# Splitting the second layer's projection weights in quarters between the projections, and GpSimd's residual steps one turn later

## The chip, the cores and the metric

The kernel runs on one core of a Trainium2 chip. The core's engines are TensorE (PE; its weight loads are listed as PEld), VectorE (DVE), ScalarE (ACT) and GpSimd (POOL); SyncE's queue (SP) issues most transfers. Each engine works through its own queue in order, and the engines wait for one another by semaphores. The metric is the device time of one execution in microseconds (us).

## The reference, cut to what matters

The network is a two-layer diffusion block on 256 latent and 256 context tokens of 1024 features. The second layer (i = 1) starts with a windowed attention with 16 query heads and 4 key/value heads of 64 features. The part that matters here is its input projection:

```python
q_lat, k_lat, v_lat = jnp.split(u_lat @ w_in, [q_cols, q_cols + kv_cols], axis=-1)
k_ctx, v_ctx = jnp.split(u_ctx @ w_in[:, q_cols:], [kv_cols], axis=-1)
q_lat = apply_axial_rope(qh(q_lat), rope_cos, rope_sin)
k_lat = apply_axial_rope(kvh(k_lat), rope_cos, rope_sin)
```

The rope is `x1 * cos - x2 * sin` and `x2 * cos + x1 * sin`. All of it is wanted in float32.

## The kernel before, in words

**Three products for one.** TensorE is given each float32 operand as a rounded high part and the rest: `mm3` (L411 to L413) multiplies high by high, high by low and low by high and adds the three in PSUM. A weight chunk `w` of 128x2048 is therefore split: ScalarE writes the high part `wh` by a copy into the rounded type (L390), VectorE subtracts it from `w` into `wl` (L391). Both come in two buffers, `wh0`/`wh1` and `wl0`/`wl1`, used in turn.

**The stage.** `inproj1` computes the projections of the second layer. The values come first. Then a loop over five chunks c (keys for c = 0, two groups of query heads for each of c = 1 to 4) runs two projections each, e = 0 and 1. A projection (`proj`) is eight k-tiles of three matmuls; k-tile kt reads columns kt*256 to kt*256+255 of the chunk, so a quarter of a chunk (512 columns) holds two k-tiles. For c = 0 a matmul is 512 wide (context and latent tokens), for the others 256.

**What follows a projection.** ScalarE moves the result out of PSUM with a scale (L2203, into `pexp`). One projection later `pend` runs the finish: for keys `k_finish`, for queries `q_finish`. A finish begins with `rope`: TensorE multiplies the moved result with a rotation matrix (L2120, into `tp`), VectorE multiplies `tp` with the sines (L2122), GpSimd the moved result with the cosines (L2123), VectorE adds the two (L2125). Then ScalarE writes the high part of the outcome (L2154 and L2155 for keys, eight pieces; L2163 for queries, two pieces) and VectorE the low part (L2157, eight pieces; L2168, two pieces). The finishes of chunk 4 are put off into the attention that follows.

**Other work in the same turns.** After each e = 1 projection `self.ada(1)` multiplies one more chunk of the modulation weights (L480 on TensorE). `steps` is a list of ten GpSimd instructions on the residual rows `N` (two of L2184, eight of L2188), which are given out two per projection.

**What sets the order.** No scheduler: instructions stand on each engine in the order in which the Python code emits them. A raw weight buffer goes back to the free list in `release`, which at once issues the next load of a fixed stream on SP's queue (`pump`, L323); that load waits there for the last reader of the buffer, and the loads behind it wait too.

Of the kernel before, what the change touches and what calls it, by code (L numbers as in the profile page):

```python
# [11 lines left out]
F32 = mybir.dt.float32  # L12
# [4 lines left out]
OP = mybir.AluOpType  # L17
# [254 lines left out]
class Kern:  # L272
# [108 lines left out]
    def split(self, pool=False, n=1, bufs=None, low=False):  # L381

        w = self.take()
        h, l = bufs or (self.part("wh"), self.part("wl"))
        for i in range(n):
            s = slice(i * 2048 // n, (i + 1) * 2048 // n)
            if pool:
                self.nc.gpsimd.tensor_scalar(h[:, s], w[:, s], 1.0, 0.0, op0=OP.mult, op1=OP.add)
            else:
                self.nc.scalar.copy(h[:, s], w[:, s])  # L390
            (self.nc.gpsimd if pool or low else self.nc.vector).tensor_tensor(l[:, s], w[:, s], h[:, s].bitcast(F32), op=OP.subtract)  # L391
        self.release()
        return h, l

    def split_steps(self, n):

        w, held = self.take(), self.held
        h, l = self.part("wh"), self.part("wl")
        for i in range(n):
            s = slice(i * 2048 // n, (i + 1) * 2048 // n)  # L400
            self.nc.gpsimd.tensor_scalar(h[:, s], w[:, s], 1.0, 0.0, op0=OP.mult, op1=OP.add)  # L401
            self.nc.gpsimd.tensor_tensor(l[:, s], w[:, s], h[:, s].bitcast(F32), op=OP.subtract)
            if i == n - 1:
                self.wq.append((h, l))
                self.release(held)
            yield
# [1704 lines left out]
    def inproj1(self, u1):  # L2111
        nc, W, d = self.nc, self.W, self.d
        cos, sin = self.rope[:, 0], self.rope[:, 1]
        rpm = self.cb[:, C_RPM:C_RPM + 128]
        lat = slice(256, 512)
        v = self.area(4, [4, 256])

        def rope(dst, src, t2=None):
            p = self.tp()
            nc.tensor.matmul(p[:, :256], rpm, src, start=True, stop=True)  # L2120
            t2 = W.tile([128, 512], F32, name="pT", bufs=4)[:, :256] if t2 is None else t2
            nc.vector.tensor_tensor(t2, p[:, :256], sin, op=OP.mult)  # L2122
            nc.gpsimd.tensor_tensor(dst, src, cos, op=OP.mult)  # L2123
            yield
            nc.vector.tensor_tensor(dst, dst, t2, op=OP.add)  # L2125
            yield

        w = self.wq.pop(0)
        for t in u1:
            uh, ul = self.uh, self.ul  # L2130
            p = self.mm()
            ts = slice(t * 128, t * 128 + 128)
            for kt in range(8):
                sl = slice(kt * 256, kt * 256 + 256)
                self.mm3(p[:, :256], (uh[kt // 4][:, kt % 4, ts], ul[kt // 4][:, kt % 4, ts]), (w[0][:, sl], w[1][:, sl]),
                         kt == 0, kt == 7)
            nc.scalar.copy(v[:, t, :], p[:, :256])

        def proj(w, off, s):
            p = self.mm()  # L2140
            for kt in range(8):
                sl = slice(kt * 256 + off, kt * 256 + off + 128)
                self.mm3(p[:, :s.stop - s.start], (w[0][:, sl], w[1][:, sl]), (uh[kt // 4][:, kt % 4, s], ul[kt // 4][:, kt % 4, s]),
                         kt == 0, kt == 7)
            return p

        def k_finish(i, s):
            r = W.tile([128, 512], F32, name="pT", bufs=4)[:, :256]
            list(rope(r, s[:, 256:512]))
            for gl in range(2):  # L2150
                g = 2 * i + gl
                q, o = slice(64 * gl, 64 * gl + 64), slice(64 - 64 * gl, 128 - 64 * gl)
                for src, ks in ((s[q, 0:256], slice(0, 256)), (r[q], lat)):
                    nc.scalar.copy(kh[q, g, ks], src)  # L2154
                    nc.scalar.copy(kh[o, g, ks], src)  # L2155
                    for dst in (q, o):
                        nc.vector.tensor_tensor(kl[dst, g, ks], src, kh[q, g, ks].bitcast(F32), op=OP.subtract)  # L2157

        def q_finish(i, s, r=None, t2=None):
            r = W.tile([128, 512], F32, name="pT", bufs=4)[:, :256] if r is None else r  # L2160
            yield from rope(r, s, t2)
            for e in range(2):
                nc.scalar.copy(q2[i // 4][64 * e:64 * e + 64, i % 4, e], r[64 * e:64 * e + 64])  # L2163
            yield
            for e in range(2):
                q, o = slice(64 * e, 64 * e + 64), slice(64 - 64 * e, 128 - 64 * e)
                z = q2[i // 4][:, i % 4, e]
                nc.vector.tensor_tensor(z[o], r[q], z[q].bitcast(F32), op=OP.subtract)  # L2168
            yield

        kh = self.area(2, [4, 512], F32R)
        kl = self.area(3, [4, 512], F32R)
        q2 = [self.area(h, [4, 2, 256], F32R) for h in range(2)]
        nxt = self.wq.pop(0)
        self.table(AF.Exp)

        steps = []
        for h in range(2):
            hs = slice(h * 512, h * 512 + 512)
            gb = self.nt(h).rearrange("p (i n) -> p i n", i=2)  # L2180
            for i, name in enumerate(("ln_g", "ln_b")):
                a = d[name][0, 1, hs]
                nc.scalar.dma_start(gb[:, i], bass.AP(tensor=a.tensor, offset=a.offset, ap=[[0, 128], [1, 512]]))
            steps.append(lambda gb=gb: nc.gpsimd.tensor_scalar(gb, gb, ALPHA, 0.0, op0=OP.mult, op1=OP.add))  # L2184
            for row in (2, 3):
                n = self.nt(row)[:, hs]
                for x, op in ((gb[:, 0], OP.mult), (gb[:, 1], OP.add)):
                    steps.append(lambda n=n, x=x, op=op: nc.gpsimd.tensor_tensor(n, n, x, op=op))  # L2188
        pend, ends = None, []
        for c in range(5):  # L2190
            w = nxt
            if c < 4:
                nxt = self.split(n=4)
            for e in range(2):
                i = 2 * (c - 1) + e
                p = proj(w, e * 128, slice(0, 512) if c == 0 else lat)
                if c < 4:
                    s = W.tile([128, 512], F32, name="pexp", bufs=5)
                    s = s if c == 0 else s[:, :256]
                else:  # L2200
                    o = W.tile([128, 1024], F32, name=("gm", "bm")[e])
                    s, r, t2 = (o[:, 256 * k:256 * k + 256] for k in range(3))
                nc.scalar.mul(s, p[:, :s.shape[1]], 0.125 if c else 1.0)  # L2203
                if e:
                    self.ada(ADA_IN1[c])
                if pend:
                    pend()
                    pend = None
                for f in steps[:2] if c else []:
                    f()  # L2210
                del steps[:2 if c else 0]
                if c == 0:
                    pend = lambda i=e, s=s: k_finish(i, s)
                elif c < 4:
                    pend = lambda i=i, s=s: list(q_finish(i, s))
                else:

                    ends.append(q_finish(i, s, r, t2))
        assert not steps
        return q2, kh, kl, v, chain(*ends)  # L2220
# [373 lines left out]
```

## Time and profile before

| | |
|---|---|
| three runs | 798.36 us median (797.3 to 800.5) |
| profiled execution | 796.03 us, of which its span, first to last instruction, is 794.2 us |
| mean granted TensorE clock | 0.955 of full speed |
| busy over the span | PE 708.4, DVE 465.5, ACT 278.5, POOL 231.4 us |
| the stage of the change | 493 to 545 us |

Busy times overlap, and a matmul's end is modelled, so the share of TensorE is not its efficiency. A wait counts only where the engine that waits is the one that the end depends on.

### The profile page before, as it was taken

What the parts mean: (1) busy time and instruction counts of PE and PEld (TensorE: products, weight loads), DVE (VectorE), ACT (ScalarE), POOL (GpSimd) and SP (SyncE); (2) the same over time, 40 slices, a digit from 0 to 9 for tenths busy, and PEclk for the clock granted to TensorE, in tenths of its full rate; (3) what the DMA queues carried; (4) which work ended last, traced back from release to release, by engine and by line L of the source; (5) the groups of instructions that cost most, each with busy time, mean ns of one, the idle gap of its engine ahead of it and who ended that gap; (6) DMA issues with size and microseconds to landing.
All of it is one profiled execution on the core that took longest, in us unless ns stands there. A gap on an engine that the chain in (4) does not pass through costs nothing. (4 is left out here: it accounts for less than half of the span.)

```text
span 794.2 us, 11447 instructions
## 1 busy us (share of the span) xinstructions
PE 708.4 (89%) x4162; PEld 413.5 (52%) x4162; DVE 465.5 (59%) x1000; ACT 278.5 (35%) x611; POOL 231.4 (29%) x250
## 2 busy tenths in 40 slices
PE   4799999979989987999999787979999978899993
PEld 0477676724567764433433247765556744454430
DVE  0589897747754877723334386587676388322115
ACT  0541212036775254110110246455768342111121
POOL 1200000037632002844000192462486540111111
PEclk8799999969999997999999999999999997999997
DMA  9974665557458368999997932557464394996892
GB/s 360 389 286 169 241 236 202 222 205 266 141 181 338 116 225 304 385 363 349 410 415 305 394 126 93 172 212 311 181 250 159 134 385 169 422 375 258 348 375 84
DMA packets 36253, 209.66 MB, mean 264 GB/s; under 512 B 4439, under 2 KB 4695, under 8 KB 15056
## 3 DMA queue, kind: packets, MB, share of 16 engines
q1 hardware_dynamic: 27888, 183.56, 59.9%
q10 hardware_dynamic: 4816, 13.85, 5.3%
q0 software_dynamic: 3472, 11.31, 3.9%
q8 instruction: 37, 0.61, 0.3%
q14 instruction: 40, 0.33, 0.1%
HBM read 197.92 MB, written 12.06 MB: 264 GB/s over the span
## 5 line engine op out<-in xcount | busy, mean ns | idle before, releaser
L631 DVE SCALAR_TENSOR_TENSOR x<-x,sm,x 128x512 f32<-128x512 f32 x120 | 90.7, 756 | 3.4
L411 PE MATMUL mm<-H,wh 128*128 128x512 f32 (+1 forms) x208 | 78.5, 377 | 1.9 <-ACT H L614 1.9
L413 PE MATMUL mm<-H,wl 128*128 128x512 f32 (+1 forms) x208 | 76.2, 366 | 0.2 <-DVE wl L391 0.2
L412 PE MATMUL mm<-L,wh 128*128 128x512 f32 (+1 forms) x208 | 76.2, 366 | 0.1
L480 PE MATMUL aux<-w,sc 128*32 128x512 f32 x368 | 54.7, 689 | 16.8 <-ACT sc L444 7.6
L391 DVE TENSOR_TENSOR wl<-w,wh 128x512 fp32r<-128x512 f32 (+1 forms) x27 | 40.0, 1515 | 22.9 <-ACT wh L390 22.7
L401 POOL TENSOR_SCALAR wh<-w 128x256 fp32r<-128x256 f32 x32 | 13.2, 413 | 118.2 <-DMA w<-wo 118.1
L411 PEld LDWEIGHTS mm<-H,wh 128*128 128x128 f32 x208 | 40.3, 194 | 13.6 <-issue 3.4
L699 DVE TENSOR_REDUCE mx<-mm 128x1 f32<-128x512 f32 (+1 forms) x64 | 39.3, 615 | 13.3 <-PE mm L786 7.3
L1836 POOL TENSOR_TENSOR yl<-ada,yh 128x512 fp32r<-128x512 f32 x12 | 15.3, 1274 | 104.6 <-ACT yh L1833 104.6
L412 PEld LDWEIGHTS mm<-L,wh 128*128 128x128 f32 x208 | 40.3, 194 | 7.4 <-DVE L L617 1.0
L413 PEld LDWEIGHTS mm<-H,wl 128*128 128x128 f32 x208 | 40.1, 193 | 7.3 <-DVE wl L391 0.8
L411 PE MATMUL mm<-wh,H 128*128 128x512 f32 x104 | 43.2, 415 | 0.0
L723 ACT COPY pT<-tp 128x512 f32<-128x512 f32 (+1 forms) x64 | 33.9, 530 | 25.4 <-PE tp L721 25.1
L412 PE MATMUL mm<-wl,H 128*128 128x512 f32 x104 | 41.1, 395 | 0.0
L1402 PE MATMUL aux<-x,H 128*32 128x512 f32 (+2 forms) x104 | 38.6, 612 | 0.0
L1508 DVE TENSOR_TENSOR y<-mm,y 128x512 f32<-128x512 f32 x18 | 12.3, 690 | 41.7 <-PE mm L1420 41.5
L390 ACT CAST wh<-w 128x512 fp32r<-128x512 f32 (+1 forms) x27 | 29.6, 1139 | 8.7 <-PE mm L413 8.5
L714 POOL TENSOR_SCALAR pexp<-pexp,ss 128x512 f32<-128x512 f32 x32 | 22.4, 701 | 31.8 <-DVE ss L713 24.7
L413 PE MATMUL mm<-wh,L 128*128 128x512 f32 x80 | 31.4, 393 | 0.0
L1830 DVE TENSOR_TENSOR ada<-pv,m 128x512 f32<-128x512 f32 x13 | 9.0, 691 | 37.7 <-PE pv L1420 37.7
L714 POOL TENSOR_SCALAR x<-x,ss 128x256 f32<-128x256 f32 (+1 forms) x32 | 21.1, 661 | 32.4 <-DVE ss L713 23.1
(471 smaller groups left out, 1703.8 us busy)
## 6 DMA issues: line engine op xcount, KB each, us to landing
w<-ada_w SPq DMA_DIRECT2D x46, 1024.0 KB, 6.9
x<-exp SPq DMA_DIRECT2D x35, 1024.0 KB, 13.5
w<-exp SPq DMA_DIRECT2D x32, 1024.0 KB, 6.5
w<-w SPq DMA_DIRECT2D x15, 1024.0 KB, 10.3
wh<-exp SPq DMA_DIRECT2D x12, 1024.0 KB, 10.2
wl<-exp SPq DMA_DIRECT2D x12, 1024.0 KB, 9.8
w<-wo SPq DMA_DIRECT2D x8, 1024.0 KB, 8.8
yd<-x ACTq DMA_DIRECT2D x1, 4096.0 KB, 17.2
```

The costliest lines, as they stand in the source:

```text
L390: self.nc.scalar.copy(h[:, s], w[:, s])
L391: (self.nc.gpsimd if pool or low else self.nc.vector).tensor_tensor(l[:, s], w[:, s], h[:, s].bitcast(F32), op=OP.subtract)
L411: t.matmul(out, ah, bh, start=start, stop=False, skip_group_check=onto)
L412: t.matmul(out, ah, bl, start=False, stop=False, skip_group_check=onto)
L413: t.matmul(out, al, bh, start=False, stop=stop, skip_group_check=onto)
L480: nc.tensor.matmul(p[32 * j:32 * j + 32, :], self.sc[:, kt, :], w[:, j * 512:(j + 1) * 512], start=(kt == 0), stop=(kt == 7), skip_group_c ...
L631: nc.vector.scalar_tensor_tensor(acc[:, i], src, w, acc[:, i], op0=OP.mult, op1=OP.add)
L699: nc.vector.reduce_max(mx, p[:, :nk], axis=AX.X, negate=True)
L714: nc.gpsimd.tensor_scalar(P[i][:, :nk], P[i][:, :nk], r[:, 0:1], 0.0, op0=OP.mult, op1=OP.add)
L723: nc.scalar.copy(T[i][:, :nk], t[:, :nk])
L1402: self.nc.tensor.matmul(p[r], x(kt)[:, r], w_j[:, kt % 4 * 512:kt % 4 * 512 + 512], start=(kt == 0), stop=(kt == 7), skip_group_check=True)
L1836: (V if u == N - 1 else nc.gpsimd).tensor_tensor(lo, y, hi.bitcast(F32), op=OP.subtract)
```

## The change

The split of the next chunk is no longer emitted whole at the top of a turn. A new helper gives it as four steps of a quarter each, and two of them are emitted behind each projection's finish. GpSimd's residual steps start with c = 2 and not with c = 1.

```diff
+    def split_parts(self, n):
+
+        w, held = self.take(), self.held
+        h, l = self.part("wh"), self.part("wl")
+
+        def step(i):
+            s = slice(i * 2048 // n, (i + 1) * 2048 // n)
+            self.nc.scalar.copy(h[:, s], w[:, s])
+            self.nc.vector.tensor_tensor(l[:, s], w[:, s], h[:, s].bitcast(F32), op=OP.subtract)
+            if i == n - 1:
+                self.release(held)
+
+        return (h, l), [lambda i=i: step(i) for i in range(n)]
...
         for c in range(5):
-            w = nxt
+            w, parts = nxt, []
             if c < 4:
-                nxt = self.split(n=4)
+                nxt, parts = self.split_parts(4)
...
                 if pend:
                     pend()
                     pend = None
-                for f in steps[:2] if c else []:
+                for f in parts[2 * e:2 * e + 2]:
+                    f()
+                for f in steps[:2] if c > 1 else []:
                     f()
-                del steps[:2 if c else 0]
+                del steps[:2 if c > 1 else 0]
```

The rows below are instructions in the order of an engine's queue, the line first; `x2` and `x4` are repeats. Lines of the changed kernel are higher by 14 to 16, since the helper stands ahead of them: L402 and L403 are its split.

VectorE, from the split of chunk 1 to the key finishes (`rope` and `x` tiles: L2122/L2136 the sines, L2125/L2139 the sum, L2157/L2171 the low parts of the keys). Before:

```order
L391 TENSOR_TENSOR wl0_6428<-w1_6139,wh0_6427 128x512 x4
L2122 TENSOR_TENSOR pT_6503<-tp_6501,rope_294 128x256
L2125 TENSOR_TENSOR pT_6500<-pT_6500,pT_6503 128x256
L2157 TENSOR_TENSOR x3_6418<-pexp_6464,x2_6417 64x256 x2
L2157 TENSOR_TENSOR x3_6418<-pT_6500,x2_6417 64x256 x2
L2157 TENSOR_TENSOR x3_6418<-pexp_6464,x2_6417 64x256 x2
L2157 TENSOR_TENSOR x3_6418<-pT_6500,x2_6417 64x256 x2
L391 TENSOR_TENSOR wl1_6524<-w2_6166,wh1_6523 128x512 x4
L2122 TENSOR_TENSOR pT_6565<-tp_6563,rope_294 128x256
```

The same place in the changed kernel:

```order
L403 TENSOR_TENSOR wl0_6428<-w1_6139,wh0_6427 128x512 x2
L2136 TENSOR_TENSOR pT_6497<-tp_6495,rope_294 128x256
L2139 TENSOR_TENSOR pT_6494<-pT_6494,pT_6497 128x256
L2171 TENSOR_TENSOR x3_6418<-pexp_6454,x2_6417 64x256 x2
L2171 TENSOR_TENSOR x3_6418<-pT_6494,x2_6417 64x256 x2
L2171 TENSOR_TENSOR x3_6418<-pexp_6454,x2_6417 64x256 x2
L2171 TENSOR_TENSOR x3_6418<-pT_6494,x2_6417 64x256 x2
L403 TENSOR_TENSOR wl0_6428<-w1_6139,wh0_6427 128x512 x2
L2136 TENSOR_TENSOR pT_6555<-tp_6553,rope_294 128x256
```

The last two quarters of chunk 1 now stand behind the first key finish, and the split of chunk 2 has left its place ahead of the second key finish.

ScalarE, while TensorE works on chunks 2 and 3 (`pexp<-mm` is the move out of PSUM, `wh` the high part of a chunk, `x0<-pT` the high part of a query group). Before:

```order
L2203 ACTIVATE pexp_6612<-mm_6587 128x256
L2163 CAST x0_6419<-pT_6620 64x256 x2
L390 CAST wh0_6633<-w1_6437 128x512 x4
L2203 ACTIVATE pexp_6670<-mm_6645 128x256
L2163 CAST x0_6419<-pT_6672 64x256 x2
L2203 ACTIVATE pexp_6710<-mm_6685 128x256
L2163 CAST x0_6419<-pT_6718 64x256 x2
L390 CAST wh1_6731<-w2_6533 128x512 x4
```

The changed kernel, from the first half of chunk 2's split on:

```order
L402 CAST wh1_6523<-w2_6166 128x512 x2
L2217 ACTIVATE pexp_6604<-mm_6579 128x256
L2177 CAST x0_6419<-pT_6612 64x256 x2
L402 CAST wh1_6523<-w2_6166 128x512 x2
L2217 ACTIVATE pexp_6656<-mm_6631 128x256
L2177 CAST x0_6419<-pT_6658 64x256 x2
L402 CAST wh0_6629<-w3_6492 128x512 x2
L2217 ACTIVATE pexp_6700<-mm_6675 128x256
L2177 CAST x0_6419<-pT_6708 64x256 x2
L402 CAST wh0_6629<-w3_6492 128x512 x2
```

Each half of a split now stands behind the two casts of a query finish, and those wait for VectorE's sum; the second half of a chunk stands ahead of the move of that chunk's own first projection.

GpSimd, from the first cosine product on. Before:

```order
L2123 TENSOR_TENSOR pT_6500<-pexp_6464,rope_294 128x256
L2123 TENSOR_TENSOR pT_6562<-pexp_6491,rope_294 128x256
L2184 TENSOR_SCALAR N0_1818<-N0_1818 128x1024
L2188 TENSOR_TENSOR N1_1819<-N1_1819,N0_1818 128x512
L2123 TENSOR_TENSOR pT_6620<-pexp_6560,rope_294 128x256
```

The changed kernel:

```order
L2137 TENSOR_TENSOR pT_6494<-pexp_6454,rope_294 128x256
L2137 TENSOR_TENSOR pT_6552<-pexp_6485,rope_294 128x256
L2137 TENSOR_TENSOR pT_6612<-pexp_6550,rope_294 128x256
L2137 TENSOR_TENSOR pT_6658<-pexp_6604,rope_294 128x256
L2198 TENSOR_SCALAR N0_1818<-N0_1818 128x1024
L2202 TENSOR_TENSOR N1_1819<-N1_1819,N0_1818 128x512
```

The residual steps come two cosine products later. On SP's queue the release of a chunk's buffer comes later too, so the loads of chunks 3 and 4 take the buffers of modulation weights instead (`w3`, `w0` in place of `w1`, `w2`); the order of the loads in the stream is the same.

## Rows read from the trace of the kernel before

**Rows 1.** The page's busy table: engine, busy us, share of the span, instructions.

```profile
PE 708.4 (89%) x4162; PEld 413.5 (52%) x4162; DVE 465.5 (59%) x1000; ACT 278.5 (35%) x611; POOL 231.4 (29%) x250
```

**Rows 2.** Waits of TensorE from 545 us to the end: who waits for whom, us in total, times, longest; the first and the last of fifteen groups, of which none names a transfer as the releaser.

```profile
PE pv L1407 <- DVE sl L1805: 2.9, 1, 2.9
...
PE pv L730 <- ACT pT L723: 0.2, 1, 0.2
```

**Rows 3.** Waits of all engines from 505 to 545 us, same columns.

```profile
ACT x L2163 <- DVE pT L2125: 13.7, 6, 4.9
...
PE tp L2120 <- ACT pexp L2203: 6.5, 3, 3.5
...
PEld mm L413 <- DVE wl L391: 0.2, 1, 0.2
```

**Rows 4.** TensorE's timeline in the stage: start, us, engine, line, operation, in brackets the idle time before it and its releaser.

```profile
504.93 0.70 PE L2120 MATMUL tp<-pexp,cb 128*128 128x256 f32 x2
505.27 0.47 PE L411 MATMUL mm<-H,wh 128*128 128x256 f32 x1
...
506.85 0.28 PE L411 MATMUL mm<-H,wh 128*128 128x256 f32 x1
...
507.07 0.28 PE L413 MATMUL mm<-H,wl 128*128 128x256 f32 x1
...
508.21 0.59 PE L2120 MATMUL tp<-pexp,cb 128*128 128x256 f32 x2
...
519.78 0.70 PE L2120 MATMUL tp<-pexp,cb 128*128 128x256 f32 x2 [3.52 <-ACT pexp L2203]
520.13 0.47 PE L411 MATMUL mm<-H,wh 128*128 128x256 f32 x1
...
524.75 1.06 PE L480 MATMUL aux<-w,sc 128*32 128x512 f32 x8
...
531.28 0.47 PE L411 MATMUL mm<-H,wh 128*128 128x256 f32 x1
...
534.38 1.06 PE L480 MATMUL aux<-w,sc 128*32 128x512 f32 x8
...
543.68 1.07 PE L480 MATMUL aux<-w,sc 128*32 128x512 f32 x8
544.68 0.50 PE L2234 MATMUL mm<-x,x 128*128 128x512 f32 x1
```

**Rows 5.** ScalarE's timeline in the stage.

```profile
506.88 0.41 ACT L2154 CAST x<-pT 64x256 fp32r<-64x256 f32 x1 [1.53 <-DVE pT L2125]
...
509.44 2.18 ACT L390 CAST wh<-w 128x512 fp32r<-128x512 f32 x4
...
519.36 0.37 ACT L2203 ACTIVATE pexp<-mm 128x256 f32<-128x256 f32 x1
...
541.43 0.83 ACT L2163 CAST x<-pT 64x256 fp32r<-64x256 f32 x2 [1.26 <-DVE pT L2125]
```

**Rows 6.** VectorE's timeline in the stage.

```profile
495.53 2.50 DVE L391 TENSOR_TENSOR wl<-w,wh 128x512 fp32r<-128x512 f32 x4 [4.36 <-ACT wh L390]
505.66 0.42 DVE L2122 TENSOR_TENSOR pT<-tp,rope 128x256 f32<-128x256 f32 x1 [7.64 <-PE tp L2120]
...
511.35 4.12 DVE L391 TENSOR_TENSOR wl<-w,wh 128x512 fp32r<-128x512 f32 x4
...
515.91 0.98 DVE L2125 TENSOR_TENSOR pT<-pT 128x256 f32<-128x256 f32 x1
...
532.58 2.40 DVE L2168 TENSOR_TENSOR x<-pT,x 64x256 fp32r<-64x256 f32 x2 [0.47 <-ACT x L2163]
...
538.47 0.43 DVE L2125 TENSOR_TENSOR pT<-pT 128x256 f32<-128x256 f32 x1
539.37 0.87 DVE L2168 TENSOR_TENSOR x<-pT,x 64x256 fp32r<-64x256 f32 x2 [0.47 <-ACT x L2163]
```

**Rows 7.** GpSimd in the stage: a row of its timeline, and its groups from 505 to 545 us (busy us, mean ns, idle before).

```profile
513.19 3.42 POOL L2188 TENSOR_TENSOR N<-N,N 128x512 f32<-128x512 f32 x2
```

```profile
L2188 POOL TENSOR_TENSOR N<-N,N 128x512 f32<-128x512 f32 x8 | 12.4, 1556 | 0.2
...
L2184 POOL TENSOR_SCALAR N<-N 128x1024 f32<-128x1024 f32 x2 | 2.3, 1140 | 0.1
```

**Rows 8.** TensorE by stretches: us, busy us and instructions, granted clock (1.00 is full speed), DMA share, GB/s.

```profile
478.00:480.00 2.00, 1.51 (x13) 1.00 0.42 90
521.00:524.20 3.20, 3.20 (x18) 0.51 0.35 143
678.00:680.00 2.00, 1.54 (x4) 0.51 1.00 418
```

**Rows 9.** TensorE's timeline where two of these stretches begin.

```profile
478.49 0.39 PE L413 MATMUL mm<-x,L 128*128 128x256 f32 x1 [3.29 <-DVE L L2064]
...
678.46 0.69 PE L1407 MATMUL pv<-cb,sl 128*128 128x128 f32 x2 [2.88 <-DVE sl L1805]
```

**Rows 10.** Loads: the issues of chunks 3 and 4 on SP's queue, and the page's row on loads of this kind (count, size, median us from issue to landing).

```profile
498.05 0.33 SPq L323 DMA_DIRECT2D w<-w  x1
...
515.50 0.33 SPq L323 DMA_DIRECT2D w<-w  x1
```

```profile
w<-w SPq DMA_DIRECT2D x15, 1024.0 KB, 10.3
```

## The prediction

> **What bounds the kernel now.** I read the page's busy table first: TensorE is busy for 708.4 of 794.2 us [rows 1]. Then the waits of TensorE behind the stage: fifteen groups, the longest 2.9 us, and none waits for a transfer [rows 2]. So behind 545 us the end follows TensorE, and what the attention's start gains or loses at 544.68 us arrives at the end almost whole. Within the stage the waits show three stops of TensorE at the rotation matmul, 6.5 us together, each for ScalarE's move of the projection (L2203) [rows 3]. ScalarE in turn stands in its query casts, 13.7 us, for VectorE's sum. TensorE waits for a split only once, 0.2 us. The timelines say why: the second move of chunk 1 comes at 519.36 us, and TensorE has been idle for 3.52 us [rows 4, 5]. Ahead of it on VectorE stands the whole split of chunk 2, 4.12 us from 511.35 us [rows 6]. After that stop TensorE runs at the half clock: 0.51 granted from 521.0 to 524.2 us [rows 8]. The projection there takes 4.62 us (520.13 to 524.75), a later one 3.10 us (531.28 to 534.38) [rows 4], so the drop costs 1.5 us. What a change in this stage can take away is thus 6.5 + 1.5 + 0.2 = 8.2 us.
>
> **The prices.** A projection in an e = 0 turn lasts 2.94 us (505.27 to 508.21). It reaches its fifth k-tile 1.58 us after its start, and there the matmul that wants the third quarter's low part 1.80 us after it [rows 4]. The e = 1 ones take 3.1 us, the modulation matmuls 1.0 us (543.68 to 544.68), a rotation 0.35 us [rows 4]. The rotation's result meets VectorE 0.73 us after its start (504.93 to 505.66), and the sine product takes 0.42 us [rows 4, 6]. The sum takes 0.43 us alone and 0.98 us where GpSimd is at work; a pair of low parts 0.87 and 2.40 us; a quarter of a split 0.62 us (2.50 / 4) and 1.03 us (4.12 / 4) [rows 6]. On ScalarE six key casts take 2.56 us (506.88 to 509.44), two query casts 0.83 us, a quarter 0.55 us (2.18 / 4) [rows 5].
>
> **What is removed.** The whole split no longer stands ahead of a finish, so the moves come when their projection ends, and the three stops at the rotation go. The quarters are the same instructions as before, sixteen on each of the two engines, so their work costs nothing new; only their place does.
>
> **What is added: a wait in the middle of a projection.** The third and fourth quarter of the next chunk stand behind the finish whose rotation TensorE issues just ahead of the projection that reads them. So each chunk's first projection waits in its fifth k-tile for a round trip: rotation, sine, sum, casts, third quarter. Alone that is 0.73 + 0.42 + 0.1 + 0.43 + 0.83 + 0.6 (a quarter to its own end) + 0.62 = about 3.7 us to the low part. TensorE gets there 0.35 + 1.80 = 2.15 us after the rotation's start. At least 1.6 us is thus lost for every chunk, wherever VectorE is. Walked through, with the times of before as the clock:
>
> Chunk 1. The first key finish has the long form. Rotation at 504.93, sine at 505.66, sum done at 506.6; six casts to 509.2; third quarter high at 509.8. VectorE has four pairs, 506.6 to 510.1, then the third quarter's low part at 510.75, the fourth at 511.4. TensorE stops from 506.85 to 509.85, then briefly, and ends at 512.0 and not at 508.2: 3.8 us.
>
> Chunk 2. The second key finish runs from there: sine at 512.7, sum done at 513.65, casts to 516.2, first quarter high at 516.9, low at 517.8 (pairs to 517.15), second 518.4. TensorE is through with the second projection, the modulation and the rotation at 516.65, so it loses 0.9 us at once. The query finish then begins on VectorE at 518.45. GpSimd's two steps fall on it, since they wait only for a cosine product that is ready at 517.7: sum 519.7, casts 520.6, third quarter high 521.2, low 522.15, fourth 522.8. TensorE ends at 523.4 and not at 519.6: 3.8 us.
>
> Chunks 3 and 4. The first two quarters are ready in time (low parts at 527.9 and 528.6, first wanted at 528.2 and 528.9). The round trip is the one above plus half a collision: the sum 0.3, the pair 0.6 longer. Chunk 3 ends at 533.6 and not at 531.0, chunk 4 2.6 us late too. The last projection, its modulation and the attention's start come at 548.3 us, against 544.68: **3.6 us later**.
>
> **Clock.** The walk has no half-clock stretch. Its stops are 3.0, 2.3 and twice 1.75 us. In this trace a stop of 2.88 us was followed by 0.51, one of 3.29 us by full clock [rows 8, 9]. I take one drop as before, 1.5 us: +5.1 us.
>
> **GpSimd's steps.** Ten instructions, 12.4 + 2.3 us [rows 7], all kept. Before, two groups of them fell on the key finishes; now none does, which saves VectorE about 1.3 us there (its first pair and sum; in the walk). They fall instead on the query finishes of chunks 2 to 4, which now stand on TensorE's path. The bounds: nothing lost in the three collisions takes 0.9 us from each, 2.7 us in all; all three at the longest rows (sum +0.55, pair +1.53, two quarters +0.82 = 2.9 each) add 2 us each, 6 us in all.
>
> The Trainium skill speaks against moving them here. Its page "SBUF — State Buffer", section "Who interferes with whom", says that a VectorE instruction with two SBUF inputs and a GpSimd instruction that reads SBUF exclude each other, whichever issues first holding the port for its whole length. The rows agree in kind (0.87 to 2.40 us for a pair), yet four quarters under 3.42 us of GpSimd work lost 1.6 us and not all of it. By the page's rule each of the two steps in a turn could hold VectorE for its whole 1.56 us, so 3.1 us a turn where the walk has 0.9: 6.6 us more, 810 us.
>
> **Loads.** Chunk 3's load was issued at 498.05, chunk 4's at 515.50 us [rows 10]. Now they wait for modulation matmuls that end at 504.9 and 516.3 us, and with 10.3 us to land [rows 10] they are there at 515 and 527 us. They are wanted at 526 and 536 us. Nothing is paid; if this cover failed, TensorE would wait in full for what is missing of it. The modulation loads behind them on SP follow the quarters (511, 523, 533 us) and have ten us or more to their product.
>
> **Sum.** 796.03 + 5.1 = 801.2 us for an execution like the profiled one. The median of the runs shown is 2.3 us above that execution, so 798.36 + 5.1 = **803.5 us**.
>
> **Rivals.** First, the change does what one would wish: the quarters are ready when their k-tile comes, and the 8.2 us go: 790 us. That needs the low part 2.15 us after the rotation; the rows add up to 3.7 us alone, so only an order other than the queue's could give it. It turns to a gain at all where the four chunks lose less than 2 us each on average; chunk 1 alone has 3.8 us. 0.05. Second, a wash: the collisions cost nothing and no clock drop follows: 3.6 - 2.7 = +0.9 us, 799.3 us. For it speaks that stops of 1.75 us may leave the clock alone; against it that GpSimd's steps have no other time to run. With the walk itself without a drop (+3.6, 802 us) it makes up the middle: 0.33. Third, all three collisions at the longest rows (+6), with or without a second clock drop (+1.5): 809.5 to 811 us; for it the 2.40 us pair, against it the quarters, which lost less. 0.12. Fourth, that the stage does not set the end and any difference is hidden behind 545 us: against it the waits there [rows 2]; its time is 798.4, and I count it in the middle with 0.02 of it.
>
> **How the numbers follow.** A difference of 0.5%, 4.0 us, is about what a measurement of this kernel can tell from no change. Slower by more than that (over 802.4 us): the walk with one drop, 0.50, and the third rival, 0.12, so 0.62. Within: 0.33. Faster: 0.05. The likeliest case alone spans 801.5 to 806.5 us. The range takes in the wash (799.3, less 1.3 for the spread of the runs) and the longest collisions (803.5 + 6): 798 to 809.5 us.
>
> **What would show it.** In the trace of the changed kernel: waits of TensorE at L2120's successor for the moves gone, and in their place waits within the projections (L425 for ScalarE's `wh`, L427 for VectorE's `wl`), 10 to 14 us together, the longest near 507 us; the casts of the query finishes directly behind sums and quarters directly behind casts; GpSimd's steps within the query finishes; attention starting at 548 to 550 us. The prediction is wrong if TensorE passes the fifth k-tiles without a wait, if the attention starts before 546 us, or if TensorE waits for chunk 3's or 4's load.

## The result: 1.1% slower

The changed kernel takes 806.75 us (median of four runs, 804.64 to 809.57) against 798.49 us (797.3 to 800.5) of the kernel before in the same series. The ratio is 1.0109, its 95% interval 1.0077 to 1.0141. The forecast was 803.5 us, 798 to 809.5.

The profiled execution took 809.57 us, the longest of the four. Its busy table answers to [rows 1]:

```profile
span 807.8 us, 11440 instructions
PE 715.6 (89%) x4162; PEld 418.6 (52%) x4162; DVE 467.9 (58%) x1000; ACT 279.2 (35%) x611; POOL 230.5 (29%) x250
```

The instruction counts of these engines are those of before. So no work was added; things stand elsewhere.

To compare the two traces I take the stage from the end of the last value copy on ScalarE to the first score matmul on TensorE. By stretches (start and end, us, TensorE's busy us and instructions, granted clock, DMA share, GB/s) that is, before:

```profile
492.90:544.70 51.80, 45.23 (x297) 0.97 0.57 203
```

and after, with three short stretches inside the stage:

```profile
498.50:559.10 60.60, 49.70 (x296) 0.92 0.51 174
518.00:520.00 2.00, 2.00 (x9) 0.50 0.86 270
542.00:544.00 2.00, 2.00 (x10) 0.50 0.82 287
552.00:554.00 2.00, 1.56 (x7) 0.50 0.15 20
```

A stretch ahead of the stage, before and after:

```profile
475.00:490.00 15.00, 9.31 (x77) 1.00 0.20 71
475.00:490.00 15.00, 9.11 (x50) 0.66 0.21 71
```

The stage is 60.6 - 51.8 = 8.8 us longer, and the medians are 8.3 us apart. Idle time of TensorE grew from 6.6 to 10.9 us, busy time by 4.5 us for the same matmuls. The three short rows say why it is busy longer: they lie in three stretches at the half clock (about 517.5 to 521, 541 to 545 and 551.5 to 555 us). Summed over pieces of 0.5 us, 10.2 us ran at the half clock, 3.4 us before. There a 256-column matmul starts about every 0.21 us, at full clock about every 0.12 us, so such a microsecond does about half the work: (10.2 - 3.4) / 2 = 3.4 us at most, since TensorE also waits in part of these stretches. Idle (4.3) and clock (3.4) make 7.7 of the 8.8 us; the rest is busy time that I cannot assign. From the first score matmul on, the remaining time is 248.7 us, 249.5 before.

The last two rows lie ahead of the change: 0.66 granted there, 1.00 before, over code that the change leaves alone. At 0.66 about 10.2 of the 15 us ran at the half clock; half of that, 5.1 us, is most of the 5.6 us by which this execution entered the stage late, and it is 13.5 us longer than the profiled one of before. The profiled executions of all the other kernels below show some of it too (0.66 to 0.89), steps_only and late_whole among them, which split as before. So it is no effect of the change, and I compare stages, not spans.

The waits of TensorE from 505 to 560 us, where [rows 3] had three stops at the rotation, 6.5 us (who waits for whom, us, times, longest):

```profile
PE mm L425 <- ACT wh L402: 8.1, 4, 2.8
PE mm L427 <- DVE wl L403: 2.7, 5, 1.3
```

No wait for the move is left, and 10.8 us of waits for the next chunk's parts have come. Behind the stage there are fifteen groups again, the longest as in [rows 2] and none for a transfer:

```profile
PE pv L1421 <- DVE sl L1819: 2.9, 1, 2.9
```

Chunk 1 shows a round trip from start to end. TensorE's timeline (start, us, line, idle time before and its releaser), which answers to [rows 4], with the later rotations (L2134):

```profile
510.56 0.70 PE L2134 MATMUL tp<-pexp,cb 128*128 128x256 f32 x2
...
515.48 0.38 PE L425 MATMUL mm<-H,wh 128*128 128x256 f32 x1 [2.81 <-ACT wh L402]
...
517.77 1.06 PE L2134 MATMUL tp<-pexp,cb 128*128 128x256 f32 x2
523.54 0.70 PE L2134 MATMUL tp<-pexp,cb 128*128 128x256 f32 x2
...
530.01 0.59 PE L2134 MATMUL tp<-pexp,cb 128*128 128x256 f32 x2
534.35 0.70 PE L2134 MATMUL tp<-pexp,cb 128*128 128x256 f32 x2
...
541.61 1.05 PE L2134 MATMUL tp<-pexp,cb 128*128 128x256 f32 x2
547.44 0.70 PE L2134 MATMUL tp<-pexp,cb 128*128 128x256 f32 x2
...
554.74 0.75 PE L2134 MATMUL tp<-pexp,cb 128*128 128x256 f32 x2
```

VectorE's timeline from there:

```profile
511.30 0.42 DVE L2136 TENSOR_TENSOR pT<-tp,rope 128x256 f32<-128x256 f32 x1 [4.59 <-PE tp L2134]
511.83 0.42 DVE L2139 TENSOR_TENSOR pT<-pT 128x256 f32<-128x256 f32 x1
...
532.16 2.40 DVE L2182 TENSOR_TENSOR x<-pT,x 64x256 fp32r<-64x256 f32 x2 [0.47 <-ACT x L2177]
534.59 1.83 DVE L403 TENSOR_TENSOR wl<-w,wh 128x512 fp32r<-128x512 f32 x2
536.34 0.41 DVE L2136 TENSOR_TENSOR pT<-tp,rope 128x256 f32<-128x256 f32 x1
536.86 0.98 DVE L2139 TENSOR_TENSOR pT<-pT 128x256 f32<-128x256 f32 x1
```

And ScalarE's:

```profile
512.28 0.41 ACT L2168 CAST x<-pT 64x256 fp32r<-64x256 f32 x1 [1.30 <-DVE pT L2139]
...
514.81 1.14 ACT L402 CAST wh<-w 128x512 fp32r<-128x512 f32 x2
```

Rotation 510.56, sine 511.30, sum 511.83, six casts from 512.28, third quarter from 514.81, and at 515.48 TensorE goes on in its fifth k-tile, after 2.81 us of standing. Before, ScalarE did the whole split ahead of the move, where [rows 5, 6] have it.

### The profile page after: what moved, and what is told of

Its sections match the earlier page's. It is cut to its first block, busy times and chain, and to the rows that moved or that the text cites. A ratio compares the mean times of both kernels' runs of the same rounds, so it can differ in the third digit from the quotient of the medians.

```text
span 807.8 us, 11440 instructions
## 1 busy us (share of the span) xinstructions
PE 715.6 (89%) x4162; PEld 418.6 (52%) x4162; DVE 467.9 (58%) x1000; ACT 279.2 (35%) x611; POOL 230.5 (29%) x250
## 5 line engine op out<-in xcount | busy, mean ns | idle before, releaser
L391 DVE TENSOR_TENSOR wl<-w,wh 128x2048 fp32r<-128x2048 f32 x11 | 25.3, 2303 | 16.9 <-ACT wh L390 16.8
L1416 PE MATMUL pv<-w,X 128*32 128x512 f32 (+2 forms) x96 | 30.1, 596 | 0.0
## 6 DMA issues: line engine op xcount, KB each, us to landing
wh<-exp SPq DMA_DIRECT2D x12, 1024.0 KB, 10.9
```

The costliest lines, as they stand in the source:

```text
L1416: self.nc.tensor.matmul(p[r], x(kt)[:, r], w_j[:, kt % 4 * 512:kt % 4 * 512 + 512], start=(kt == 0), stop=(kt == 7), skip_group_check=True)
```

## The experiments

All use the changed kernel or the one before as a base, and all ratios are to the kernel before in the same series (medians there 798.41, 799.47 and 798.64 us). A ratio can differ from the quotient of the medians by a quarter of a per cent (no_steps). "Stage" is the stretch defined above, "half" the sum of its time at the half clock, "rest" the time from the first score matmul to the last instruction; these are of the one profiled execution of each kernel.

| kernel | split / GpSimd's steps | median us (runs) | ratio, 95% interval | stage | idle | half | rest |
|---|---|---|---|---|---|---|---|
| before | whole, ahead / from c = 1 | 798.4 (27) | | 51.8 | 6.6 | 3.4 | 249.5 |
| after | quarters behind each finish / from c = 2 | 806.75 (4) | 1.0109 (1.0077 to 1.0141) | 60.6 | 10.9 | 10.2 | 248.7 |
| quarters_only | as after / from c = 1 | 808.95 (5) | 1.0134 (1.0094 to 1.0175) | 65.4 | 11.9 | 20.5 | 249.8 |
| steps_only | as before / from c = 2 | 799.64 (11) | 1.0007 (0.9982 to 1.0032) | 50.3 | 4.9 | 3.4 | 249.5 |
| second_ahead | 3rd and 4th quarter ahead of the finish / from c = 2 | 802.85 (11) | 1.0038 (1.0012 to 1.0064) | 54.6 | 7.5 | 3.4 | 249.5 |
| all_first | four quarters behind the e = 0 finish / from c = 2 | 800.66 (11) | 1.0024 (1.0000 to 1.0049) | 53.1 | 6.3 | 3.4 | 249.3 |
| no_steps | as after / none | 801.63 (10) | 1.0051 (1.0029 to 1.0072) | 54.8 | 7.4 | 6.8 | 248.5 |
| filler | as after, idle matmuls / from c = 2 | 806.0 (5) | 1.0093 (1.0058 to 1.0128) | 60.1 | 6.8 | 3.4 | 248.3 |
| early_whole | as before / five at c = 0, five in the attention | 792.77 (5) | 0.9910 (0.9875 to 0.9945) | 45.7 | 2.7 | 0 | 249.2 |
| early_all_first | as all_first / as early_whole | 797.46 (11) | 0.9980 (0.9960 to 1.0000) | 48.9 | 4.1 | 3.4 | 249.9 |
| late_second_ahead | as second_ahead / all in the attention | 797.66 (11) | 0.9981 (0.9954 to 1.0008) | 46.8 | 2.2 | 3.4 | 252.8 |
| late_all_first | as all_first / all in the attention | 795.8 (11) | 0.9964 (0.9937 to 0.9991) | 46.2 | 1.5 | 3.4 | 252.0 |
| late_whole | as before / all in the attention | 795.02 (11) | 0.9958 (0.9934 to 0.9983) | 44.3 | 1.4 | 0 | 252.1 |

### The two parts alone

The change without the later steps (quarters_only, against after):

```diff
-                for f in steps[:2] if c > 1 else []:
+                for f in steps[:2] if c else []:
                     f()
-                del steps[:2 if c > 1 else 0]
+                del steps[:2 if c else 0]
```

> The quarters behind the finishes, but GpSimd's residual steps from c = 1 on as before: one half of the change alone. Theory A (the round trip of quarters behind the finish that TensorE's own rotation starts is the cost): the waits for wh and wl inside the first projection of chunks 1 to 4 stay, 10 us or more together, and the kernel is slower than the one before by 5 to 11 us; the collisions fall on the key finish of chunk 1 and less on chunk 4. Theory B (the later place of GpSimd's steps is the cost): within 2 us of the kernel before. Theory C (the cost is the clock drops alone, from any stop): slower by 1.5 us for each half-clock stretch in the stage and no more.

Measured 1.0134. TensorE's waits in its stage and the stage's row by stretches:

```profile
PE mm L425 <- ACT wh L402: 8.4, 5, 3.1
PE mm L427 <- DVE wl L403: 3.5, 4, 1.5
```

```profile
497.10:562.50 65.40, 53.52 (x296) 0.84 0.47 161
```

The waits are those of the changed kernel, a little longer, and the half clock takes 20.5 us here. The order of the quarters makes the loss by itself. This execution is the slowest of the five (814.15 us), and in its stage, 13.6 us longer than before, the clock is the larger part: (20.5 - 3.4) / 2 = 8.5 us at most, against 5.3 us of idle time. So it does not say how waits and clock share the loss in the median of runs.

The later steps without the quarters (steps_only) are the reverse edit on the kernel before.

> The whole split at the top of the turn as before, but GpSimd's residual steps from c = 2 on: the other half of the change alone. Theory A: no wait of TensorE for wh or wl inside a projection above 0.3 us; the split of chunk 2 takes about 2.5 and not 4.12 us and the first key pair 0.87 and not 1.94, so the second move of chunk 1 comes some 2 to 3 us earlier and the stop of 3.5 us shrinks below 1.5 us; the later query finishes take the collisions: between 4 us faster and 1 us slower than before. Theory B: slower by 5 us or more.

Measured 1.0007, no difference that can be told; the stage is 1.5 us shorter. The split of chunk 2 takes 3.04 us on VectorE and not 4.12 [rows 6] (2.5 expected), and the stops at the rotation fall from 6.5 to 4.5 us, the longest from 3.5 to 1.9 (below 1.5 expected):

```profile
PE tp L2120 <- ACT pexp L2203: 4.5, 4, 1.9
```

The later steps are not the cause of the loss.

### The round trip taken away by another place

In second_ahead the third and fourth quarter go ahead of the e = 1 finish, and no longer wait for its sum and casts:

```diff
+                for f in parts[2:] if e else []:
+                    f()
                 if pend:
                     pend()
                     pend = None
-                for f in parts[2 * e:2 * e + 2]:
+                for f in [] if e else parts[:2]:
                     f()
```

> As the change, but the third and fourth quarter stand ahead of the finish of the e = 1 turn and not behind it, so that they no longer wait for the rotation that TensorE issues just ahead of the projection that reads them. Theory A: the waits inside projections fall below 1.5 us in all, no wait at the rotation comes back above 2 us, and the kernel is 2 to 7 us faster than the one before. Theory D (VectorE has too much to do in this stage whatever the order, so the wait only moves): waits of TensorE in the stage of 6 us or more, time within 3 us of the kernel before.

It came out at 1.0038, slower than before and not faster. The stage is 6.0 us shorter than after's (3.4 us of idle time and 2.6 of busy time, with two half-clock stretches fewer), so the place behind the finish did cost; but other waits came. TensorE's waits in the stage, and a piece of VectorE's and GpSimd's timelines:

```profile
PE mm L427 <- DVE wl L403: 5.6, 9, 1.2
PE mm L425 <- ACT wh L402: 1.9, 1, 1.9
```

```profile
526.98 4.96 DVE L403 TENSOR_TENSOR wl<-w,wh 128x512 fp32r<-128x512 f32 x4
```

```profile
528.22 1.72 POOL L2202 TENSOR_TENSOR N<-N,N 128x512 f32<-128x512 f32 x1
529.91 1.49 POOL L2198 TENSOR_SCALAR N<-N 128x1024 f32<-128x1024 f32 x1
```

Four quarters stand together there and take 4.96 us, 2.50 alone [rows 6]: the loss of 2.46 us lies beside 3.2 us of GpSimd work. TensorE now waits for the low parts.

All four quarters behind the e = 0 finish (all_first) give them a turn more:

```diff
-                for f in parts[2 * e:2 * e + 2]:
+                for f in [] if e else parts:
```

> As the change, but all four quarters stand behind the finish of the e = 0 turn. Theory A: every quarter is ready a projection ahead of its use; no waits inside projections, and moves wait for at most two casts: 2 to 7 us faster than before. Theory D: the split of four quarters ahead of the second finish delays that finish's casts and the next move as before, waits at the rotation of 4 us or more, within 3 us of the kernel before.

Measured 1.0024, at the edge of a difference, so not the gain of theory A; nor are there the waits at the rotation that theory D wanted. The waits for low parts stay (5.1 us, nine times), those for high parts fall to 1.1. In this kernel as well the four quarters took 4.96 and 5.20 us.

### The collisions taken away

In no_steps the ten residual steps are left out of the changed kernel:

```diff
-                for f in steps[:2] if c > 1 else []:
-                    f()
-                del steps[:2 if c > 1 else 0]
+                steps.clear()
```

> The changed kernel with GpSimd's ten residual instructions left out of the stage (the residual rows are then not scaled, part of the computation is missing). Nothing of GpSimd but the cosine products then meets VectorE there. Theory A (the round trip alone costs most): the waits for wh and wl within projections stay at 7 to 10 us of the 10.9 us of idle time that the stage has with the steps, and the kernel stays 2 to 7 us slower than the one before. Theory E (the collisions in the new place cost most): the waits fall below 5 us and the time to within 2 us of the kernel before.

Measured 1.0051. The stage falls from 60.6 to 54.8 us. VectorE's groups in the stage (busy us, mean ns, idle before them) say how. After:

```profile
L403 DVE TENSOR_TENSOR wl<-w,wh 128x512 fp32r<-128x512 f32 x16 | 11.6, 768 | 8.8 <-ACT wh L402 8.6
L2182 DVE TENSOR_TENSOR x<-pT,x 64x256 fp32r<-64x256 f32 x12 | 9.1, 762 | 3.0 <-ACT x L2177 2.8
L2139 DVE TENSOR_TENSOR pT<-pT 128x256 f32<-128x256 f32 x8 | 5.6, 702 | 0.8
```

Without the steps:

```profile
L403 DVE TENSOR_TENSOR wl<-w,wh 128x512 fp32r<-128x512 f32 x16 | 10.6, 701 | 9.7 <-ACT wh L402 9.6
L2182 DVE TENSOR_TENSOR x<-pT,x 64x256 fp32r<-64x256 f32 x12 | 5.0, 420 | 3.0 <-ACT x L2177 2.8
L2139 DVE TENSOR_TENSOR pT<-pT 128x256 f32<-128x256 f32 x8 | 3.7, 463 | 0.8
```

VectorE is stretched by 1.0 + 4.1 + 1.9 = 7.0 us, and the stage by 5.8: 3.5 us of idle time, and busy time of which one half-clock stretch explains up to (10.2 - 6.8) / 2 = 1.7. The round trip stays, though, with GpSimd out of its way:

```profile
PE mm L425 <- ACT wh L402: 6.6, 4, 2.8
PE mm L427 <- DVE wl L403: 0.7, 3, 0.2
```

Those 7.3 us are waits of the order alone, and the kernel is still slower than the one before, whose stage holds the steps.

### The clock

In filler, TensorE is kept busy where it would stand: six extra matmuls of 512 columns ahead of the fifth k-tile of each query chunk's first projection.

```diff
+                if kt == 4 and fill:
+                    z = self.pv()
+                    for _ in range(fill):
+                        nc.tensor.matmul(z, w[0][:, :128], uh[0][:, 0], start=True, stop=True)
...
-                p = proj(w, e * 128, slice(0, 512) if c == 0 else lat)
+                p = proj(w, e * 128, slice(0, 512) if c == 0 else lat, 6 if c and not e else 0)
```

> The changed kernel with six matmuls of 512 columns more, with no reader, ahead of the fifth k-tile of the first projection of chunks 1 to 4: about 1.4 us of extra work for TensorE at full clock, put where it waits. Theory F (the half-clock stretches that follow the stops are a third or more of the loss): the stretches in the stage fall from about 10 us to 4 us or less and the time by 2 to 4 us, to 802 to 805 us, though there is more to do. Rival: the stretches stay as they are, or the time does not fall: then the extra work costs up to 4 times 1.4 us or nothing, 806 to 812 us.

Measured 806.0 us, not to be told from the changed kernel; theory F's 802 to 805 us did not come. The time at the half clock fell from 10.2 to 3.4 us and the idle time from 10.9 to 6.8, as expected of the clock; the 24 extra matmuls take 24 x 0.233 = 5.6 us themselves. Clock (3.4) and idle time (4.1) should give back 7.5, so 1.9 us should be left as a gain; the stage shows 0.5. That the drops hang on the stops fits this one execution; it is not shown, since the number of drops also changes from one execution to the next, and their price in time is not settled by it.

### GpSimd's steps out of the stage

Five steps go ahead of the queries and five into the attention, first with the split of before (early_whole, against the kernel before):

```diff
-                for f in steps[:2] if c else []:
+                for f in [] if c or e else steps[:5]:
                     f()
-                del steps[:2 if c else 0]
+                del steps[:0 if c or e else 5]
...
-        assert not steps
+        self.rsteps = steps
...
+            if i and self.rsteps:
+                self.rsteps.pop(0)()
```

> The order of the kernel before (whole split at the top of a turn), but five of GpSimd's residual steps at the first turn, where VectorE idles, and five in the attention behind. The collisions with splits and finishes go. If VectorE's load in the stage is what the waits come from (theory D), its splits take 2.5 us each, TensorE's idle time in the stage falls from 6.6 us to 3 us or less, no half-clock stretch, 2 to 6 us faster than before. If not, within 2 us of before; slower by up to 3 us if the five steps in the attention hold up its scalings on GpSimd.

Measured 792.77 us, 0.9910 (0.9875 to 0.9945): faster than both kernels. TensorE's waits in the stage, its row by stretches, and GpSimd's first steps:

```profile
PE tp L2120 <- ACT pexp L2203: 2.7, 3, 1.7
```

```profile
497.00:542.70 45.70, 42.96 (x296) 1.00 0.64 231
```

```profile
504.17 1.07 POOL L2184 TENSOR_SCALAR N<-N 128x1024 f32<-128x1024 f32 x1 [9.78 <-DMA N<-ln_b]
505.32 5.26 POOL L2188 TENSOR_TENSOR N<-N,N 128x512 f32<-128x512 f32 x4
510.53 1.44 POOL L2123 TENSOR_TENSOR pT<-pexp,rope 128x256 f32<-128x256 f32 x2
```

The whole split takes 2.50 us on VectorE (chunk 2's 3.03, beside a cosine product), the stops for the moves fall from 6.5 to 2.7 us, and the granted clock is full throughout. The last block shows what the early steps cost: the first step stood 9.78 us for a load of its rows, and the first cosine product waits behind the steps until 510.53 us.

The same steps with all four quarters behind the e = 0 finish (early_all_first):

> All four quarters behind the finish of the e = 0 turn, and the residual steps as in the run above. Theory D: without collisions the quarters take 2.5 us, are ready ahead of their projection, and nothing waits: 3 to 7 us faster than before, idle time of TensorE in the stage under 3 us. If the order of the split still matters more than VectorE's load, the waits for wl at the start of a chunk stay above 3 us and the time is within 2 us of before.

Measured 0.9980 (0.9960 to 1.0000), not to be told from before. TensorE stood 3.71 us at chunk 2's first k-tile:

```profile
520.00 0.38 PE L425 MATMUL mm<-H,wh 128*128 128x256 f32 x1 [3.71 <-ACT wh L402]
```

That high part stands behind the second key finish, and this behind the first, whose sum waited for that late cosine product. Here the whole split at the top of a turn beats the quarters, since it waits for no finish.

### The round trip with no collisions in the way

Two orders of quarters without GpSimd's steps in the stage: late_second_ahead has the order of second_ahead, late_all_first that of all_first, and late_whole the split of before. All ten steps go into the attention through the hook of early_whole.

> Quarters as in the change, but the third and fourth ahead of the finish and not behind it, and all ten residual steps in the attention behind the stage, where nothing of them meets VectorE's splits. Beside the run without steps (stage 54.8 us) the place of two quarters is what differs. Theory G (the round trip through the finish is what the change's order costs): the waits for wh and wl of 7.3 us fall to 2.5 us or less, the stage takes 45 to 49 us and the time is 2 to 6 us below the kernel before. Rival H (quarters between the finishes cost, wherever they stand): stage 51 us or more, time not faster.

> All four quarters behind the finish of the e = 0 turn, all ten residual steps in the attention. Theory G: stage 45 to 48 us, 3 to 7 us faster than before; the stop of 3.7 us at chunk 2 of the run with early steps shrinks below 2 us, since it came from a cosine product that waited behind steps at the first turn. Rival H as above.

> The order of the kernel before with all ten residual steps in the attention. If the stage is set by VectorE's load, it takes 44 to 46 us as with five steps at the first turn or a little less, and the time is 5 to 8 us below the kernel before; if ten steps in the attention hold up its scalings on GpSimd, the attention gives 2 us or more of it back.

late_second_ahead and no_steps differ in the stage by nothing but the place of the third and fourth quarter. TensorE's waits there, and the row by stretches:

```profile
PE mm L425 <- ACT wh L402: 1.9, 1, 1.9
PE mm L427 <- DVE wl L403: 0.3, 1, 0.3
```

```profile
496.20:543.00 46.80, 44.59 (x296) 0.96 0.63 225
```

2.2 us of waits in place of 7.3, and a stage of 46.8 us in place of 54.8: the round trip costs 8.0 us, 5.1 of them idle time, the rest busy time, of which the clock explains 1.7 (half: 6.8 to 3.4). These are single executions, but the medians agree: no_steps lies 2.2 us above the kernel before of its series, late_second_ahead 1.0 us below, although its rest is 4.3 us longer. The expectation for the whole kernel, 2 to 6 us faster than before, was missed: 0.9981 (0.9954 to 1.0008). The rest has grown from 249.5 to 252.8 us with the steps in the attention. A part of it is a wait for GpSimd's scalings there, in the kernel before and in late_whole:

```profile
PE tp L721 <- POOL pexp L714: 0.6, 2, 0.4
PE tp L721 <- POOL pexp L714: 1.4, 3, 0.6
```

late_all_first (0.9964) and late_whole (0.9958) pay about 2.5 us in the rest as well and keep a little, 2.8 and 3.6 us by the medians, less than the 3 to 7 and 5 to 8 expected. late_whole has the shortest stage of all, 44.3 us, within its 44 to 46.

## Why the prediction was right, point by point

**Direction and mechanism: right.** The three stops at the rotation are gone, and in their place TensorE waits, almost always in the fifth k-tile of the first projections, 10.8 us (10 to 14 foretold), the longest at chunk 1, 2.81 us (3.0 foretold). quarters_only, no_steps and late_second_ahead show that the round trip makes it. Its price holds too: without the steps (no_steps) chunk 3 uses the third quarter's low part 533.76 - 529.78 = 4.0 us after the rotation's start, where the sum had 3.7.

**Size: 8.3 us, or 8.8 in the stage, against 5.1.** From rotation to rotation, chunk 1's first projection took 517.77 - 510.56 = 7.2 us (walked 7.1), chunk 2's 6.5 (walked 7.1), chunks 3's and 4's 7.3 each (walked 5.9): 2.3 us over the walk in all. The second projections of chunks 1 and 3 took 5.8 us each where 4.35 was walked, at the half clock: 2.9 us where one drop, 1.5, was allowed. 5.1 + 2.3 + 1.4 = 8.8. The median, 806.75 us, lies in the range but just above the 801.5 to 806.5 us of the likeliest case. That the range held it is partly luck: its upper end had room for longer collisions with one drop, and most of the excess is clock.

**The terms that were too small.** The clock first: three stretches and not one. Two cost 2.9 us in the second projections. The third lies in chunk 4's first one, whose end runs at 0.50:

```profile
540.24 0.39 PE L427 MATMUL mm<-H,wl 128*128 128x256 f32 x1 [0.35 <-DVE wl L403]
...
552.44 0.58 PE L427 MATMUL mm<-H,wl 128*128 128x256 f32 x1 [0.48 <-DVE wl L403]
```

From this matmul to the next rotation chunk 3 needs 541.61 - 540.24 = 1.4 us, chunk 4 554.74 - 552.44 = 2.3: another 0.9. Together 3.8 us of clock where 1.5 stood in the sum, 2.3 too few. The other 1.4 us are waits, and come mainly from chunk 3: the walk gave it half a collision, 0.9 us, but the pair (2.40) and the quarters (1.83) ahead of it held its sine to 536.34 us, 1.99 us behind the rotation and not 0.73, and the sum took 0.98. That is 1.8 us. Chunk 2 lost 0.6 us less than walked.

By the rule of the Trainium skill's page "SBUF — State Buffer", section "Who interferes with whom", the prediction estimated that GpSimd's steps could hold VectorE for 3.1 us a turn. The steps stand in five turns, and three of these fall on the first projections of chunks 2 to 4. VectorE's instructions lost 7.0 / 5 = 1.4 us a turn (no_steps), less than half of 3.1, and 2.46 beside 3.2 us of steps in second_ahead, some three quarters: in kind the page's rule, in size less. On TensorE's path there arrived 10.9 - 7.4 = 3.5 us of idle time; if all of it belongs to the three first projections, that is 1.2 each, nearer to the walk's 0.9.

**The walk's other parts.** GpSimd's steps fell on the query finishes, as said. The loads of chunks 3 and 4 were there: no matmul waits for a transfer. The attention's start carried through one to one: the rest is 248.7 us and was 249.5. It began 8.8 us later in the stage's terms, where 3.6 to 5.1 were foretold.

**The rivals.** The 8.2 us gain could not come: the wait for the quarters is there in every order that puts them behind their own finish. The wash fell with the clock and the collisions. The third, all collisions at their longest with a second drop, came nearest in kind; its 809.5 to 811 us was too high, since only chunk 3 came near its price. The fourth fell too: the 8.8 us of the stage arrive at the end. What neither the walk nor a rival held is how much the steps cost the kernel before already: early_whole, without them, is 51.8 - 45.7 = 6.1 us shorter in the stage.

**Open.** What part of the 8.3 us is the clock's own in the median of runs: in filler the drops were fewer and the time was not measurably less. And why code ahead of the stage, which the change leaves alone, ran partly at the half clock in every profiled execution but that of the kernel before.

## What to carry to other kernels

An operand that is prepared behind a finish on in-order queues comes a whole round trip (matmul, two VectorE steps, casts) after the matmul that starts that finish; put the preparation ahead of the finish whose matmul directly precedes its user, or a full turn earlier. Splitting one long stretch of work into pieces gains only if each piece waits for less than the whole did. And before moving such work, look at what else stretches it: here no order of the split that was tried gained on the kernel before while GpSimd's ten steps stood in the stage, and taking the steps out of it did.

## What the runs showed of the hardware

- **The length of a stop alone did not tell whether the clock fell.** Stops of 2.81 and 2.18 us in the changed kernel were followed by the half clock (0.50 granted from 518 and from 542 us), and one of 1.86 us, which ended at 551.37, by 0.50 from 552; in all_first one of 1.14 us, which ended at 518.54, by 0.50 from 521; before, one of 3.29 us was not [rows 8, 9]. The same code ahead of the stage ran at 0.66 granted in one execution and 1.00 in another.
- **VectorE's low parts of a chunk took 2.50 us alone, 3.0 beside cosine products, 3.9 to 5.5 us beside GpSimd's residual steps** (3.88 and 4.96 in second_ahead, 4.12 before, 5.54 in early_all_first), four instructions of the same size each time.
- **Work that is taken from a stage is not free in the next**: the ten steps in the attention gave back 2.5 to 3.3 us of the 7 to 8 that they had cost in the stage.
